# Loading four row tiles of x before w_out and keeping half of the residual on chip in the MLP of a one-layer hybrid attention block

## The chip, the cores and the metric

The kernel runs on one core of a Trainium2 chip. A core has a matrix engine (TensorE, PE in the profile, with its weight loads as PEld), a vector engine (VectorE, DVE), a scalar engine (ScalarE, ACT), GpSimd (POOL) and SyncE (SP, which here only issues DMAs). Each takes its instructions in the order of the program, and they wait for each other by semaphores. On-chip memory is SBUF; matrix products land in PSUM, which has 8 banks of 128 x 512 float32. The metric is the device time of one execution in microseconds, lower is better. Before the change it is 2884.75 us, the median of 3 runs (2883.74 to 2885.79).

## The reference

One layer of a decoder block in float32, 512 positions of 2048 features:

```python
xn = rmsnorm(x, g_mix)
(q_a, k_c, ..., c_q, c_kv, k_r, gate_a, gate_b) = split(xn @ w_in)
o_a = nsa_attention(...)          # 16 heads, compressed, selected and windowed keys
o_b = mla_attention(...)          # 16 heads, low-rank queries and keys
mixed = sigmoid(gate_a) * (o_a @ w_o_nsa) + sigmoid(gate_b) * (o_b @ w_o_mla)
h = x + mixed @ w_out
h = h + memory_cross_attention(rmsnorm(h, g_xattn), rmsnorm(mem, g_mem))   # 4 heads, 256 tokens
h = h + square(relu(rmsnorm(h, g_mlp) @ w_ff1)) @ w_ff2                    # 2048 -> 8192 -> 2048
return rmsnorm(h, g_final)
```

Every matrix is read from memory once, in float32. The change touches `mixed @ w_out`, the cross-attention's output projection, and the MLP.

## The kernel before

**Products.** Each float32 operand is split into a high and a low part in a reduced format. A product is three matmuls: high by high, high by low, low by high (L395 to L397 in the attention stages, L1606 to L1608 in w_out and the MLP). ACT makes the high part by a cast (L402, L1428), DVE the low part by a subtraction (L403, L1433).

**Stages, in order.** The input projection with the first attention, the second attention with the gates (both up to about 1100 us), then `mix` (L1152): the product with w_o_nsa, the memory's keys and values, and a loop over d = 0 to 15 with w_o_mla (L1186 to L1196). Then `Out.run` (L1832), the product with w_out; `cross` (L1280), the cross-attention, whose last part is a loop over four column blocks f of the output projection with four steps k each (L1330 to L1360); and `Mlp.run` (L1529), first w_ff1 (layer 1), then w_ff2 (layer 2).

**The seven products.** w_out and both MLP layers use a fast 2 x 2 block scheme: 7 products instead of 8 for each chunk of weights. w_out has 2 chunks (products p = 0 to 13), each MLP layer 8 chunks (p = 0 to 55 and 56 to 111). A product has four units j = 0 to 3, and a unit is one weight tile of 128 x 1024 (512 KB) with 12 matmuls. Unit i = 4p + j. What a product needs:

- Its weights. `load` (L1407): products n = 0, 3, 5 of a chunk load a tile plainly by SP (L1416). Products 1, 2, 4, 6 add the next block onto the tile that is already there, by an accumulating DMA of POOL (L1423). Such a load can start only when the low part of the unit four before has been made from the same tile.
- High and low parts of the weights: `high` on ACT (L1428), `low` on DVE (L1433).
- Its stationary side S: a sum of activation blocks, made by DVE (`add`, L1470, lines L1474 to L1480), and S's high and low part (`stat` and `stat_low`: ACT L1501, DVE L1506; in w_out L1811 and L1816).

`prep(i)` (L1442) sets the order: loads up to i + 5, high parts up to i + 2, low parts up to i + 1. It is called with i + 3 at unit i. `ahead(step)` makes the same preparations for the first units, in four steps, before the first product starts. In w_out these are called at d = 12 to 15 of the w_o_mla loop (L1195), in the MLP at k = 0 to 3 of the last column block (L1357).

**PSUM.** Four banks are named mm, three st, one o. In w_out the set X is st and o, the set Y is mm. In MLP layer 1 (two banks in a set) X is mm and Y is st (L1544, L1546). The four column blocks of the output projection each use all four mm banks; DVE empties them into the residual at L1349.

**The residual.** h is held as eight tiles `R[t, b]` (four row tiles t, two column halves b) of 128 x 1024. `Out.run` loads x into them by SP (`Out.res_in`, L1828 to L1830): two ahead of the first product, the other six at j = 2 and 3 of products 0 to 2 (L1855). The output projection adds to them. Then:

- `x_in(d)` (L1656) turns the residual to features by four PE transposes (L1261) into an st bank and scales it into the MLP's input, half by ACT (L1659) and half by DVE (L1660). d = 0 to 11 come in the column blocks f = 1 to 3, d = 12 to 15 in product 0 of the MLP (L1567).
- `square(t, q)` (L1743) adds up squares for the norm on ACT, for a row tile and a quarter of the columns.
- `res_out(b)` (L1662) stores four tiles to memory with DMAs issued by ACT (L1664). b = 0 is stored at f = 2, k = 2, b = 1 in product 0 at j = 1. All eight come back by SP in products 39 to 53 (`res_in`, L1678 to L1680).

**Slots.** Nearly everything lives in 40 slots of 128 x 1024 (`Slots`), plus a few lent areas (the tiles named d and PP in the profile). `get` takes the slot that has been free the longest, so an instruction that fills a slot waits for its former readers. Scratch for squares and for u is six half slots (L1397).

**The u transposes.** The MLP's inner result is turned by PE (L1672) into the bank o, copied by ACT (L1673) and stored (L1674), in jobs spread over the next two products.

Of the kernel before, what the change touches and what calls it, by code (L numbers as in the profile page):

```python
# [9 lines left out]
F32 = mybir.dt.float32  # L10
# [344 lines left out]
class Layer:  # L355
    def __init__(self, tc, ctx, a, order, info):
# [17 lines left out]
        self.d_r = dr.tile([4, 2, 128, 1024], F32, name="d_r")  # L374
# [777 lines left out]
    def mix(self):  # L1152
# [32 lines left out]
        out = None  # L1185
        for d in range(KT):  # L1186
            ps = self.ft("wm", d, M)
            g = st[d % 4]
            nc.vector.scalar_tensor_tensor(g, g, 1.0, ps, op0=OP.add, op1=OP.mult)
            nc.vector.tensor_add(self.RES[d], self.RES[d], g)  # L1190
            sig(KT + d + 3)
            if d == 9:
                out = Out(self)
                out.loads(4)
            if d >= 12:  # L1195
                out.ahead(d - 12)  # L1196
# [83 lines left out]
    def cross(self, rate, out):  # L1280
# [49 lines left out]
        for f in range(4):  # L1330
            ps = [self.new_mm() for _ in range(4)]
            for h in range(2):
                w = self.W.get(("xo", f, h))
                for kk in range(2):
# [5 lines left out]
                    for t in range(4):  # L1340
# [4 lines left out]
                        if f and 0 < k < 3 and t % 2:  # L1345
                            mlp.x_in(4 * f + 2 * k - 6 + t // 2)
# [3 lines left out]
                    if f and k == 0:  # L1350
                        for t in range(4):
                            mlp.square(t, f - 1)
                    if f == 2 and k == 2:
                        mlp.res_out(0)
                    if f == 2 and k == 3:
                        mlp.loads(4)
                    if f == 3:  # L1357
                        mlp.ahead(k)
# [7 lines left out]
class Mlp:  # L1366
# [19 lines left out]
    def begin(self, k):  # L1386
# [3 lines left out]
        self.nl = self.nh = self.no = self.ns = 0  # L1390
        self.units = 4 * (self.NP + 7 * self.CH)

    def __init__(self, k):
# [3 lines left out]
        self.us, self.usl = k.halves(6)  # L1397
# [131 lines left out]
    def run(self, out):  # L1529
# [8 lines left out]
        back = deque((t, b) for b, ts in ((0, (0, 1)), (1, (2, 3, 0, 1)), (0, (2, 3))) for t in ts)  # L1538
        for p in range(last):
# [3 lines left out]
            if n == 0:  # L1543
                X = [k.new_mm() for _ in range(nb)]  # L1544
            if n in (1, 5):
                Y = [k.new_st() for _ in range(min(nb, 3))] + [k.new_o() for _ in range(nb - 3)]  # L1546
            ps = (X, Y)[which]
            nh = 1 if p + 1 >= self.NP else 2
            for j in range(4):
# [4 lines left out]
                if j == 1 and back and p > self.NP - 18 and p % 2:  # L1554
                    self.res_in(*back.popleft())
# [9 lines left out]
                if p == 0 and j < 2:  # L1565
                    for d in (0, 1):
                        self.x_in(12 + 2 * j + d)  # L1567
                    if j:
                        for t in range(4):
                            self.square(t, 3)  # L1570
                        self.res_out(1)
                if p == 2 and j == 1:
# [79 lines left out]
    def scratch(self):  # L1652
        self.ns = (self.ns + 1) % 2
        return self.us[4 + self.ns]

    def x_in(self, d):  # L1656
        k, nc = self.k, self.nc
        ps, g = k.to_features(d, k.new_st()), k.gains[:, G_MLP + d:G_MLP + d + 1]
# [3 lines left out]
    def res_out(self, b):  # L1662
        for t in range(4):
            self.nc.scalar.dma_start(self.k.d_r[t, b], self.R[t, b])  # L1664
            self.k.put(self.R.pop((t, b)))
# [12 lines left out]
    def res_in(self, t, b):  # L1678
        self.R[t, b] = self.k.slots.plain()
        self.nc.sync.dma_start(self.R[t, b], self.k.d_r[t, b])  # L1680
# [62 lines left out]
    def square(self, t, q):  # L1743
        self.nc.scalar.activation(self.scratch(), self.row(t, q), AF.Square,
# [27 lines left out]
class Out(Mlp):  # L1772
# [6 lines left out]
    def __init__(self, k):  # L1779
# [5 lines left out]
        self.us = [None] * 4 + [self.own[:, :512], self.own[:, :512]]  # L1785
        self.cols = self.own[:, 512:]
# [41 lines left out]
    def res_in(self, t, b):  # L1828
# [3 lines left out]
    def run(self):  # L1832
# [3 lines left out]
        rows = deque((t, b) for a, b in ((0, 0), (1, 1), (0, 1), (1, 0)) for t in (2 * a, 2 * a + 1))  # L1836
        for _ in range(2):
            self.res_in(*rows.popleft())
        X = Y = None
        for p in range(last + 1):  # L1840
# [6 lines left out]
            for j in range(4):  # L1847
# [7 lines left out]
                if rows and j > 1 and p != 3 and p != 4:  # L1855
                    self.res_in(*rows.popleft())
# [76 lines left out]
```

## Time and profile before

| | us |
|---|---|
| median of 3 runs | 2884.75 (2883.74 to 2885.79) |
| the profiled execution | 2884.82 |
| its span, first to last instruction | 2883.0 |
| mean granted clock of TensorE | 0.997 of full speed |
| TensorE (matmul) busy | 2829.2, 98% |
| VectorE busy | 1927.7, 67% |
| ScalarE busy | 1488.0, 52% |
| GpSimd busy | 385.5, 13% |
| moved by DMA | 459.06 MB, mean 159 GB/s |

The durations in the profile are of one execution. A row of a group gives line, engine, operation, tile written and read, and count. In a row of waits, the engine and what it was about to do stand left of the arrow, what it waited for stands right, then the total, the number of times and the longest in us. A DMA has an issue on its engine's queue and lands later. Matmuls are pipelined, so two neighbours overlap in the records and the busy time of TensorE counts a stream without holes as full.

### The profile page before, as it was taken

The page shows a single profiled execution, that of the slowest core. Times are in us where ns is not written, and L with a number is a line of the kernel's source. Part 1 is how long each engine was busy: PE and PEld are TensorE (multiplying, and loading weights), DVE is VectorE, ACT ScalarE, POOL GpSimd, SP SyncE. Part 2 cuts the span into 40 slices and gives each one's busy share as a digit, 9 for nine tenths or more (in the row PEclk, how much of TensorE's full clock was granted, in tenths as well). Part 3 has the DMA queues.
Part 4 walks back from the last instruction along what each step waited for, and adds up shares of the span by engine and source line. Part 5 has one row for each costly group of instructions (what it writes and reads, how often), then busy time and mean ns, then how long its engine had stood idle before and what let it go on. Part 6 is the DMA issues. An engine that isn't in the chain of part 4 may idle for free. (4 is left out here: it accounts for less than half of the span.)

```text
span 2883.0 us, 37043 instructions
## 1 busy us (share of the span) xinstructions
PE 2829.2 (98%) x13594; PEld 2357.0 (82%) x13594; DVE 1927.7 (67%) x3208; ACT 1488.0 (52%) x2574; POOL 385.5 (13%) x606
## 2 busy tenths in 40 slices
PE   9999999999999999999999999999999999999998
PEld 7878888888888888887887778888887888888886
DVE  6446766655555565457866777777766778888888
ACT  5435555654454444333555566666666544444445
POOL 3121011001010002001200111111111111111110
PEclk9999999999999999999999999999999999999999
DMA  5231111122223335558823788988899888899986
GB/s 175 88 94 61 56 57 59 61 86 98 95 99 99 95 125 195 178 186 229 205 63 110 175 206 204 221 200 200 224 224 241 223 217 224 225 232 226 230 221 163
DMA packets 149141, 459.06 MB, mean 159 GB/s; under 512 B 15840, under 2 KB 32352, under 8 KB 148960
## 3 DMA queue, kind: packets, MB, share of 16 engines
q0 software_dynamic: 41472, 151.01, 27.9%
q1 hardware_dynamic: 81872, 271.88, 27.7%
q10 hardware_dynamic: 25616, 33.82, 3.3%
q8 instruction: 106, 1.74, 0.2%
q14 instruction: 75, 0.61, 0.1%
HBM read 418.90 MB, written 37.75 MB: 158 GB/s over the span
## 5 line engine op out<-in xcount | busy, mean ns | idle before, releaser
L395 PE MATMUL mm<-s,s 128*128 128x512 f32 (+5 forms) x1528 | 609.1, 399 | 9.7 <-ACT s L402 5.8
L397 PE MATMUL mm<-s,s 128*128 128x512 f32 (+5 forms) x1528 | 585.0, 383 | 0.0
L396 PE MATMUL mm<-s,s 128*128 128x512 f32 (+5 forms) x1528 | 584.5, 383 | 0.1
L403 DVE TENSOR_TENSOR s<-s,s 128x512 fp32r<-128x512 f32 (+4 forms) x446 | 304.8, 700 | 228.8 <-ACT s L402 227.2
L1433 DVE TENSOR_TENSOR s<-d,s 128x1024 fp32r<-128x1024 f32 x281 | 339.7, 1222 | 173.4 <-ACT s L1428 173.3
L1606 PE MATMUL mm<-s,s 128*128 128x512 f32 x1120 | 440.8, 394 | 3.3 <-ACT s L1501 2.0
L1428 ACT CAST s<-d 128x1024 fp32r<-128x1024 f32 x281 | 289.4, 1050 | 297.2 <-DMA d<-wts 265.7
L1607 PE MATMUL mm<-s,s 128*128 128x512 f32 x1120 | 436.8, 390 | 1.9 <-DVE s L1433 1.8
L1608 PE MATMUL mm<-s,s 128*128 128x512 f32 x1120 | 437.4, 391 | 1.1 <-DVE s L1506 0.6
L402 ACT CAST s<-s 128x512 fp32r<-128x512 f32 (+4 forms) x446 | 264.1, 608 | 203.9 <-PE mm L396 80.5
L395 PEld LDWEIGHTS mm<-s,s 128*128 128x128 f32 x1528 | 289.4, 189 | 56.5 <-ACT s L402 6.1
L397 PEld LDWEIGHTS mm<-s,s 128*128 128x128 f32 x1528 | 288.1, 189 | 53.8
L396 PEld LDWEIGHTS mm<-s,s 128*128 128x128 f32 x1528 | 289.9, 190 | 37.7 <-DVE s L403 0.9
L1606 PE MATMUL st<-s,s 128*128 128x512 f32 x768 | 301.2, 392 | 0.8 <-ACT s L1811 0.8
L1607 PE MATMUL st<-s,s 128*128 128x512 f32 x768 | 299.2, 390 | 1.5 <-DVE s L1433 1.5
L1608 PE MATMUL st<-s,s 128*128 128x512 f32 x768 | 299.3, 390 | 0.6 <-DVE s L1816 0.6
L1423 POOL DMA_DIRECT2D d<-wts x193 | 168.5, 873 | 872.7 <-DVE s L1433 449.2
L1433 DVE TENSOR_TENSOR s<-s,s 128x1024 fp32r<-128x1024 f32 x185 | 223.4, 1221 | 82.6 <-ACT s L1428 79.3
L1428 ACT CAST s<-s 128x1024 fp32r<-128x1024 f32 x185 | 190.3, 1049 | 143.7 <-DMA s<-wts 127.7
L543 ACT ACTIVATE PP<-PP,mx 128x512 f32<-128x512 f32 (+1 forms) x208 | 116.4, 560 | 278.9 <-DVE mx L542 278.8
L1606 PEld LDWEIGHTS mm<-s,s 128*128 128x128 f32 x1120 | 210.8, 188 | 46.6 <-ACT s L1501 2.4
L1608 PEld LDWEIGHTS mm<-s,s 128*128 128x128 f32 x1120 | 210.6, 188 | 46.4 <-DVE s L1506 1.5
(298 smaller groups left out, 4254.0 us busy)
## 6 DMA issues: line engine op xcount, KB each, us to landing
s<-wts SPq DMA_DIRECT2D x286, 512.0 KB, 3.7
d<-wts POOLq DMA_DIRECT2D x193, 512.0 KB, 9.6
d<-wts SPq DMA_DIRECT2D x88, 512.0 KB, 5.7
s<-wts POOLq DMA_DIRECT2D x70, 512.0 KB, 7.9
d_u<-s ACTq DMA_DIRECT2D x64, 256.0 KB, 5.5
d<-d_u SPq DMA_DIRECT2D x26, 512.0 KB, 5.7
PP<-wts POOLq DMA_DIRECT2D x25, 512.0 KB, 9.6
d_g<-s ACTq DMA_DIRECT2D x32, 256.0 KB, 2.0
```

The costliest lines, as they stand in the source:

```text
L395: t.matmul(ps, a.hr, b.hr, start=first, stop=False)
L396: t.matmul(ps, a.hr, b.lr, start=False, stop=False)
L397: t.matmul(ps, a.lr, b.hr, start=False, stop=last)
L402: nc.scalar.copy(o.hr, src)
L403: nc.vector.tensor_sub(o.lr, src, o.hi)
L543: nc.scalar.activation(p, p, AF.Exp, bias=mx, scale=-1.0, accum_out=sm)
L1423: self.nc.gpsimd.dma_start(t, src, accum_op=OP.add)
L1428: self.nc.scalar.copy(t.hr, self.raw[i])
L1433: self.nc.vector.tensor_sub(t.lr, r, t.hi)
L1606: m(ps, a.hr, b.hr, start=first, stop=False, skip_group_check=True)
L1607: m(ps, a.hr, b.lr, start=False, stop=False, skip_group_check=True)
L1608: m(ps, a.lr, b.hr, start=False, stop=last, skip_group_check=True)
```

## The change

- **w_out.** `Out.res_in` becomes `row_in`. Four of the eight loads of x are issued in the w_o_mla loop, at d = 10, 11, 13 and 14, and the other four at j = 3 of products 0 to 3.
- **Stores.** Only the halves b = 0 are stored and loaded back. The four stores are issued by SP, one each at f = 2, k = 2 and 3, and f = 3, k = 0 and 1. The halves b = 1 keep their slots. The four reloads stay in products 47, 49, 51 and 53.
- **First preparations.** The first four weight tiles of the MLP are loaded at f = 1, k = 3 instead of f = 2, k = 3; `ahead` runs at f = 2, k = 3 and f = 3, k = 0 to 2, one k step sooner.
- **Banks.** In the first chunk of layer 1 X is st and Y is mm. The four `x_in` in product 0 use mm banks.
- **Squares.** Two of the third quarter's squares move from f = 3 to product 0, the four of the last quarter from product 0 to product 1; their sum is taken one unit later. The scratch is `rbc`, which is free by then, and the half slots go from six to four.

The diff, cut to its core:

```diff
-        self.d_r = dr.tile([4, 2, 128, 1024], F32, name="d_r")
+        self.d_r = dr.tile([4, 128, 1024], F32, name="d_r")
...
+            if d in (10, 11, 13, 14):
+                out.row_in()
             if d >= 12:
                 out.ahead(d - 12)
...
-                            mlp.x_in(4 * f + 2 * k - 6 + t // 2)
+                            mlp.x_in(4 * f + 2 * k - 6 + t // 2, self.new_st())
...
                     if f and k == 0:
-                        for t in range(4):
+                        for t in range(4 if f < 3 else 2):
                             mlp.square(t, f - 1)
-                    if f == 2 and k == 2:
-                        mlp.res_out(0)
-                    if f == 2 and k == 3:
+                    if f == 2 and k > 1 or f == 3 and k < 2:
+                        mlp.res_out((k - 2) % 4)
+                    if f == 1 and k == 3:
                         mlp.loads(4)
-                    if f == 3:
-                        mlp.ahead(k)
+                    if f == 2 and k == 3 or f == 3 and k < 3:
+                        mlp.ahead((k + 1) % 4)
...
-        self.us, self.usl = k.halves(6)
+        self.us, self.usl = k.halves(4)
+        self.sq = k.rbc
...
-                X = [k.new_mm() for _ in range(nb)]
+                X = [k.new_mm() if p else k.new_st() for _ in range(nb)]
             if n in (1, 5):
-                Y = [k.new_st() for _ in range(min(nb, 3))] + [k.new_o() for _ in range(nb - 3)]
+                Y = [k.new_st() if p > 6 else k.new_mm() for _ in range(min(nb, 3))] + [k.new_o() for _ in range(nb - 3)]
...
-                if j == 1 and back and p > self.NP - 18 and p % 2:
-                    self.res_in(*back.popleft())
+                if j == 1 and p in (self.NP - 9, self.NP - 7, self.NP - 5, self.NP - 3):
+                    self.res_in((p - self.NP + 9) // 2)
...
-                        self.x_in(12 + 2 * j + d)
-                    if j:
-                        for t in range(4):
-                            self.square(t, 3)
-                        self.res_out(1)
-                if p == 2 and j == 1:
+                        self.x_in(12 + 2 * j + d, k.new_mm())
+                if p == 0 and j == 3:
+                    self.square(2, 2)
+                    self.square(3, 2)
+                if p == 1:
+                    self.square(j, 3)
+                if p == 2 and j == 2:
                     self.r = self.rstd(range(4), "rx3")
...
-    def res_out(self, b):
-        for t in range(4):
-            self.nc.scalar.dma_start(self.k.d_r[t, b], self.R[t, b])
-            self.k.put(self.R.pop((t, b)))
+    def res_out(self, t):
+        self.nc.sync.dma_start(self.k.d_r[t], self.R[t, 0])
+        self.k.put(self.R.pop((t, 0)))
...
-        rows = deque((t, b) for a, b in ((0, 0), (1, 1), (0, 1), (1, 0)) for t in (2 * a, 2 * a + 1))
-        for _ in range(2):
-            self.res_in(*rows.popleft())
...
-                if rows and j > 1 and p != 3 and p != 4:
-                    self.res_in(*rows.popleft())
+                if p < 4 and j == 3:
+                    self.row_in()
```

More of the change, by code (lines that the diff above doesn't have):

```diff
@@ L1389, in begin @@
         self.S, self.sums, self.m = {}, {}, None
[L1390 removed]
+        self.nl = self.nh = self.no = 0
         self.units = 4 * (self.NP + 7 * self.CH)
@@ L1537, in run @@
         last = 2 * self.NP - 1
-        back = deque((t, b) for b, ts in ((0, (0, 1)), (1, (2, 3, 0, 1)), (0, (2, 3))) for t in ts)
         for p in range(last):
@@ L1650, in half, with x_in @@
         return self.us[self.nu % 4]
[L1652 to L1656, printed above, removed]
+    def x_in(self, d, ps):
         k, nc = self.k, self.nc
-        ps, g = k.to_features(d, k.new_st()), k.gains[:, G_MLP + d:G_MLP + d + 1]
+        ps, g = k.to_features(d, ps), k.gains[:, G_MLP + d:G_MLP + d + 1]
         nc.scalar.activation(self.x(d, 0), ps[:, :256], AF.Copy, scale=g)
         nc.vector.tensor_scalar(self.x(d, 1), ps[:, 256:], g, None, op0=OP.mult)
-    def res_out(self, b):
-        for t in range(4):
-            self.nc.scalar.dma_start(self.k.d_r[t, b], self.R[t, b])
-            self.k.put(self.R.pop((t, b)))
+    def res_out(self, t):
+        self.nc.sync.dma_start(self.k.d_r[t], self.R[t, 0])
+        self.k.put(self.R.pop((t, 0)))
     def u_T(self, c, b, j, cs, last):
@@ L1676, in u_T, with res_in @@
             k.put(*cs)
-    def res_in(self, t, b):
-        self.R[t, b] = self.k.slots.plain()
-        self.nc.sync.dma_start(self.R[t, b], self.k.d_r[t, b])
+    def res_in(self, t):
+        self.R[t, 0] = self.k.slots.plain()
+        self.nc.sync.dma_start(self.R[t, 0], self.k.d_r[t])
     def row(self, t, q):
@@ L1743, in square @@
     def square(self, t, q):
-        self.nc.scalar.activation(self.scratch(), self.row(t, q), AF.Square,
+        self.nc.scalar.activation(self.sq, self.row(t, q), AF.Square,
                                   accum_out=self.cols[:, 4 * t + q:4 * t + q + 1])
@@ L1784, in __init__ @@
         self.own = k.slots.get()
-        self.us = [None] * 4 + [self.own[:, :512], self.own[:, :512]]
-        self.cols = self.own[:, 512:]
+        self.sq, self.cols = self.own[:, :512], self.own[:, 512:]
+        self.rows = deque((t, b) for a, b in ((0, 0), (1, 1), (0, 1), (1, 0)) for t in (2 * a, 2 * a + 1))
     def finish(self):
@@ L1826, in ahead, with row_in @@
         self.prep(step - 1)
-    def res_in(self, t, b):
+    def row_in(self):
+        t, b = self.rows.popleft()
         self.R[t, b] = self.k.slots.get()
```

## The prediction

> **What bounds the kernel now.** I read the page first, for who is busy, then a table by stretches, to see where the matmul stream has holes, then the waits of TensorE in those stretches, and last the timelines of the engines it waited for. From the page:
>
> ```profile
> span 2883.0 us, 37043 instructions
> PE 2829.2 (98%) x13594; PEld 2357.0 (82%) x13594; DVE 1927.7 (67%) x3208; ACT 1488.0 (52%) x2574; POOL 385.5 (13%) x606
> q0 software_dynamic: 41472, 151.01, 27.9%
> q1 hardware_dynamic: 81872, 271.88, 27.7%
> ```
>
> TensorE is the bound: it is idle for 2883.0 - 2829.2 = 53.8 us, and the change takes no matmul away. So all it can win is holes, in the stages that it touches. The two queue lines give the price of a 512 KB transfer. POOL's accumulating loads: 27.9% of 2883.0 us is 804 us for 151.01 MB, that is 2.8 us of all 16 DMA engines each. Plain ones: 799 us for 271.88 MB, 1.54 us each.
>
> The stretches (columns: length, busy time and instructions of each engine, granted clock, DMA share, GB/s):
>
> ```profile
> 1285.00:1305.00 20.00, 20.00 (x90) 16.57 (x89) 11.40 (x18) 8.16 (x11) 0.00 (x0) 1.00 0.43 147
> 1305.00:1345.00 40.00, 37.79 (x162) 29.68 (x161) 25.94 (x31) 12.05 (x13) 7.12 (x8) 1.00 1.00 271
> 1330.00:1350.00 20.00, 16.70 (x66) 11.70 (x65) 14.22 (x15) 8.75 (x9) 1.74 (x2) 1.00 0.87 262
> 1400.00:1450.00 50.00, 50.00 (x222) 41.42 (x221) 42.15 (x45) 25.19 (x33) 9.63 (x11) 1.00 0.91 211
> 1580.00:1590.00 10.00, 9.38 (x38) 7.60 (x39) 3.42 (x7) 6.00 (x13) 0.00 (x0) 0.83 0.17 68
> 1600.00:1630.00 30.00, 26.91 (x120) 21.02 (x118) 18.41 (x19) 13.96 (x24) 5.23 (x6) 1.00 0.98 253
> 1630.00:1640.00 10.00, 8.30 (x28) 6.47 (x29) 7.84 (x12) 8.12 (x11) 0.86 (x1) 0.83 0.13 15
> ```
>
> An undisturbed stretch of w_out is 1400 to 1450: 222 matmuls in 50 us, 0.225 us each. Between 1330 and 1350, early in w_out, there are 66 where 20 / 0.225 = 88.8 would fit: 22.8 x 0.225 = 5.1 us lost. The second place is the end of the cross-attention's output projection and the first products of the MLP, 1578 to 1660. There two stretches also have a granted clock of 0.83: 10 x 0.17 = 1.7 us each, 3.4 us. What TensorE waited for, in w_out (1328 to 1352):
>
> ```profile
> PE st L1607 <- DVE s L1433: 1.5, 2, 0.8
> PE st L1606 <- ACT s L1811: 0.8, 1, 0.8
> PE st L1608 <- DVE s L1816: 0.6, 1, 0.6
> PE mm L1608 <- DVE s L1816: 0.3, 1, 0.3
> ```
>
> and from 1575 to 1665:
>
> ```profile
> PE mm L395 <- DVE s L1349: 2.2, 1, 2.2
> PE mm L1606 <- ACT s L1501: 2.0, 1, 2.0
> PE mm L1606 <- DVE s L1349: 1.2, 1, 1.2
> PE st L1261 <- DVE d L1660: 1.2, 1, 1.2
> PE mm L1607 <- DVE s L1433: 1.1, 2, 0.8
> PE mm L1608 <- DVE s L1506: 0.6, 1, 0.6
> ```
>
> In w_out the waits are 3.2 us in 5 gaps and the loss 5.1, so a gap costs its length and up to 0.4 us of emptying and refilling. In the second place the waits are 8.3 us in 7 gaps, the low clock 3.4, and for the refilling I take 0.2 each, 1.4: 13.1 us.
>
> **The change, part by part.**
>
> Four row tiles ahead of w_out. All 8 loads of x now fall into the stretch where the DMA engines are full. The loads, ACT's waits from 1310 to 1346, and the landing of POOL's accumulating loads (L1423) in it:
>
> ```profile
> L1830 SPq DMA_DIRECT2D s<-xr x8: 328/355/488, 1310.4 to 1341.2; - x8
> ```
>
> ```profile
> ACT s L1428 <- DMA d<-wts: 14.5, 4, 5.7
> ACT s L1428 <- DMA PP<-wts: 6.9, 2, 5.1
> ```
>
> ```profile
> DMA to landing us min/median/max: 7.3/11.2/14.4
> ```
>
> ACT waits 21.4 us for accumulated weights, and TensorE's four kinds of wait stand behind that queue: L1433 and L1816 on DVE and L1811 on ACT come after L1428 in program order. From 1305 to 1345 the share is 1.00, and the eight rows take 8 x 1.54 = 12.3 us of these 40. Four of them move to d = 10, 11, 13, 14 of the w_o_mla loop, about 1282 to 1306, where the share is 0.43; the fifth to eighth go one to a product, so that the last two fall behind 1340. On SP they stand behind gate loads that are already waiting there, and the slots they take were freed before that loop began (by the code's order of gets and puts). Behind a later row that waits for a slot stand the plain weight loads of the fourth product, which are asked for 8 units (21.6 us) ahead. So 6.2 us leave the full stretch for certain and up to 3 more go to its end, against 5.1 us of lateness. I take 4.6 of 5.1 (bounds: 2.5, if the accumulating loads stay late because each waits for its predecessor's L1433; 5.1). Extra cost in the earlier stage: 6.2 us of DMA time into 0.57 x 20 = 11.4 us of free time, nothing.
>
> Stores off ACT. Before, four d_r stores are issued by ACT in the third column block (timelines of ACT, then DVE):
>
> ```profile
> 1575.68 2.91 ACTq L1664 DMA_DIRECT2D d_r<-s  x4
> 1578.63 0.62 ACT L402 CAST s<-s 128x512 fp32r<-128x512 f32 x1 [2.48 <-issue]
> ```
>
> ```profile
> 1579.28 0.69 DVE L403 TENSOR_TENSOR s<-s,s 128x512 fp32r<-128x512 f32 x1 [2.61 <-ACT s L402]
> ```
>
> Four issues hold ACT for 2.91 us, the weight split at L402 waits, DVE's L403 waits for that, and the evacuation at L1349 stands behind L403: that is the 2.2 us wait of L395. After it the clock is 0.83. With SP issuing the stores one at a time this chain is gone. SP has only weight loads behind it there, and the stored halves have been complete for a column block. Worth 2.2 + 1.7 + 0.2 = 4.1 us (bounds: 2.4, without the clock; 4.1).
>
> Banks. The first product takes st banks, which no L1349 evacuates: the 1.2 us wait of L1606 goes, 1.4 with refilling. The four x_in transposes inside product 0 take mm banks, four of them instead of three that are reused: the 1.2 us of L1261 goes, 1.4. Products 1 to 6 then use mm for Y; these banks are emptied in product 0, whose 48 matmuls take 10.8 us. What is late next is DVE. This is its row for the low parts:
>
> ```profile
> L1433 DVE TENSOR_TENSOR s<-d,s 128x1024 fp32r<-128x1024 f32 x281 | 339.7, 1222 | 173.4 <-ACT s L1428 173.3
> ```
>
> Product 0 holds eight operations of this size on DVE (four lows, two sums, two low parts of S), 9.8 us, and eight of at most half of it (four L1349, four x_in), at most 4.9: 14.7 us against 10.8 and the transposes. Lows are made three units ahead, 3 x 12 x 0.225 = 8.1 us, which covers the 4 us. Nothing added; 4 us if that lead is used up.
>
> First preparations sooner, second four stores dropped. In products 1 and 2 the chain is the same as in w_out. Landing of POOL's loads issued 1590 to 1597, then of those issued 1605 to 1622, and the stores:
>
> ```profile
> DMA to landing us min/median/max: 5.4/5.7/5.9
> ```
>
> ```profile
> DMA to landing us min/median/max: 11.9/13.5/14.9
> ```
>
> ```profile
> d_r<-s ACTq DMA_DIRECT2D x4, 512.0 KB, 17.0
> ```
>
> The loads need 13.5 us where the first two needed 5.7, at a DMA share of 0.98, and four stores (6.2 us) are in the same stretch. After the change these stores do not exist, the first weights come a column block (10.8 us) earlier, and the accumulating loads one k step (12 matmuls, 2.7 us) earlier against product 0. ACT also loses four issues and two of four squares from product 0; four squares go to product 1, one to a unit. What this chain costs is the waits of L1606 for L1501, of L1607 and of L1608, the second low clock, and 0.2 for each of four gaps: 2.0 + 1.1 + 0.6 + 1.7 + 0.8 = 6.2 us; I take 5.3 off (bounds 2.5 and 6.2). The one scratch for all squares is written by ACT alone, in order, and rstd, one unit later, is first used at the end of product 3: nothing.
>
> Half of the residual kept. Four reloads fewer before layer 2 and the same number of stores saved above. TensorE's waits from 1665 to 2260 are mainly these:
>
> ```profile
> PE o L1672 <- ACT s L1673: 8.7, 9, 2.2
> ```
>
> ```profile
> ACT s L1428 <- DMA d<-wts: 42.3, 25, 4.0
> ACT s L1428 <- PE mm L1608: 1.9, 1, 1.9
> ```
>
> ```profile
> 2199.50 0.44 PE L1672 MATMUL o<-cst,PP 128*128 128x128 f32 x2 [2.25 <-ACT s L1673]
> ```
>
> ```profile
> 2200.00:2205.00 5.00, 5.00 (x24) 4.13 (x23) 2.48 (x3) 3.86 (x6) 0.00 (x0) 1.00 0.52 162
> ```
>
> (The ACT lines are from 1700 to 2050; then one matmul group of the timeline, and the stretch behind it.) The u transposes wait because ACT's copy stands behind an accumulated load. The remaining four reloads stay where the biggest of them is, at 2199, so I credit 0.4 us (bounds: -3, if three slots fewer in hand delay something in each of 8 column chunks; +2).
>
> Sum: 4.6 + 4.1 + 1.4 + 1.4 + 5.3 + 0.4 = 17.2 us. The profiled execution took 2884.82 us with its span of 2883.0, so 1.8 us lie around the span, and the median of the three runs is 2884.75. The span becomes 2865.8, the time 2867.6.
>
> **The rivals.**
>
> Smaller gain, DMA still binding. If the accumulating loads are late for their order (each waits for the low part of the unit four before) and not for traffic, w_out gives 2.5 and the MLP's start 2.5: 17.2 - 2.1 - 2.8 = 12.3, time 2872.5. For it: POOL's landings rise to 14.4 us. Against: from 1400 on the order is the same, with no hole.
>
> Given back. TensorE arrives 17 us earlier at products whose u transposes already wait. If each of the 8 chunks loses 0.7 us more, 5.6 us return: 2873.2. For it: ACT's 42.3 us of waits for accumulated weights. Against: the start of a chunk does not depend on when the stage began.
>
> The low clock stays. The 2.2 us gap at 1578 is followed by a clock of 0.83, but the 2.25 us gap before 2199.50 by one of 1.00. If the low stretches are not the gaps' doing, 3.4 us stay: 2871.0. The Trainium skill ("TensorE: Matmul & The Clock Gate", Part 1) lets the clock fall after at least one idle window of about 3.4 us, longer than any gap here; by that rule the sum would be 13.8 and this rival would hold. The trace speaks against it, since both low stretches begin right at a gap of about 2 us.
>
> Slower, by lack of slots. Kept rows take four slots and the scratch gives one back. Counting the code's gets and puts, 8 slots of 40 are free in products 2 to 4 of each chunk before; that becomes 5, and 3 in the first chunk. It decides when the slot that a unit four places ahead gets was last read by the unit just before TensorE's own. Twelve such units in 8 chunks at 0.3 us would be 29 us: 2896.4. The Trainium skill ("Perfetto Trace Analysis", Optimization Strategy) reads the same gap repeating as too few buffers, and would look for it here. Against it: w_out's second chunk goes down to 2 free slots by the same count and shows 222 matmuls in 50 us (1400 to 1450), and ACT waited only once for TensorE to free a slot from 1700 to 2050, 1.9 us.
>
> The change does not do what it says: SP's stores stand behind its other loads, the four early rows wait for slots, and what remains is the banks' 2.8 us: 2882.
>
> **How the numbers follow.** Forecast 0.56; DMA still binding 0.14; given back 0.12; low clock 0.08; nothing but banks 0.06; slower 0.04. A measurement of this kernel tells about 0.2% from no change, 5.8 us. All cases but the last two are faster by more: 0.90; same 0.06; slower 0.04. The range: at its best 5.1 + 4.1 + 2.8 + 6.2 + 2 = 20.2 us, 2864.6, and 1 us more for gaps I have priced low, 2863.5; at the other end the cases down to 2873.2 with 2 us for two of them together, 2875.5.
>
> **What would show it.** Right: L1830 starts near 1282 and has four issues before 1307; from 1330 to 1350 some 88 matmuls; no wait of L395 for L1349 near 1578; no granted clock under 1 from 1570 to 1640; no L1261 wait for L1660; landings of POOL's loads in product 1 under 10 us; the L1672 waits still about 8 us. Wrong: L1672's waits over 14 us, ACT's L1428 waiting for L1608 in every chunk, a new wait of L395 in the w_o_mla loop for late weights, or TensorE's first MLP matmul waiting for L1660 on the st banks.

## The result, and the profile after

The changed kernel takes 2866.07 us, the median of four runs (2863.43 to 2869.15); the kernel before took 2884.31 us beside it. The ratio is 0.9933, 95% interval [0.9922, 0.9945]: 19.3 us less, between 15.9 and 22.5. The profiled execution took 2866.99 us with a span of 2865.2, 17.8 us shorter than the span before. The forecast was 17.2 us.

From the page of the changed kernel:

```profile
span 2865.2 us, 37061 instructions
PE 2824.7 (99%) x13594; PEld 2358.1 (82%) x13594; DVE 1929.0 (67%) x3208; ACT 1488.9 (52%) x2574; POOL 384.2 (13%) x606
```

TensorE is idle for 40.5 us, 53.8 before. The rest of the gain is in its busy time, 4.5 us less: records of matmuls that run at a low clock, or whose start is held back, count as busy. So I also count the loss in another way: for every 128 x 512 matmul, how much later than 0.2267 us the next one starts, summed by stretch. This count is worked out from the timelines of TensorE and used below for all kernels:

| lost time, us | before | changed | difference | over all kernels | forecast |
|---|---|---|---|---|---|
| 1300 to 1500, w_out | 6.56 | 5.28 | 1.3 | 0.4 | 4.6 |
| 1560 to 1665, output projection and first MLP products | 14.55 | 1.94 | 12.6 | 11.2 | 12.2 |
| 1665 to 2280, rest of layer 1 | 17.36 | 13.69 | 3.7 | 7.3 | 0.4 |
| all else | 41.19 | 42.89 | -1.7 | not compared | 0 |

Two profiles are one execution each, and the count of a stretch in which nothing was edited moves by 1 to 3 us from one to the next. The twelve experiments below give more of them, so the fifth column compares means. In w_out, six kernels without the edit lose 6.39 to 6.73 (mean 6.55), four with it 5.06 to 7.72 (6.20). From 1560 to 1665, four kernels with none of the edits there lose 11.48 to 14.55 (13.18), five with all of them 1.94 to 2.03 (2.00). In the rest of layer 1, four with all slots in hand lose 17.36 to 21.10 (19.27), seven with three slots fewer 10.71 to 13.69 (11.98). That sums to 18.9 us, beside the 19.3 measured. (In the two profiles alone the four rows sum to 15.9 of the 17.8 us; the rest lies in what the count leaves out, such as the smaller matmuls.) The means also hold stretches of low clock, some 1.5 us each, which come in some executions and not in others: from none to two in the four kernels of 13.18, and one in w_out in one of the four of 6.20.

So the total came out as forecast, and one of its three parts did. w_out gave almost nothing of its 4.6 us, and layer 1 gave about 7 where 0.4 was forecast.

The stretches of the changed kernel, with the columns of the forecast's table:

```profile
1285.00:1305.00 20.00, 20.00 (x89) 16.55 (x89) 11.13 (x16) 8.79 (x12) 0.00 (x0) 1.00 0.69 242
1305.00:1345.00 40.00, 38.79 (x170) 31.43 (x169) 28.78 (x33) 12.96 (x13) 7.10 (x8) 1.00 0.90 237
1330.00:1350.00 20.00, 18.45 (x79) 14.27 (x78) 14.27 (x15) 10.01 (x10) 2.53 (x3) 1.00 0.73 195
1580.00:1590.00 10.00, 10.00 (x53) 8.28 (x53) 5.58 (x8) 5.74 (x9) 1.75 (x2) 1.00 0.37 56
1600.00:1630.00 30.00, 30.00 (x134) 24.85 (x133) 25.03 (x29) 22.86 (x36) 5.27 (x7) 1.00 0.77 170
1630.00:1640.00 10.00, 10.00 (x46) 8.29 (x45) 9.96 (x10) 4.35 (x5) 3.47 (x4) 1.00 0.96 202
```

Three stretches are whole now: 53 matmuls where there were 38, 134 for 120, 46 for 28, and both low clocks (0.83) are gone. From 1330 to 1350 there are 79, not the 88 that I had named as the sign of a closed hole. What TensorE still waits for, first in w_out (1328 to 1385), then from 1665 to 2260; from 1545 to 1665 the view lists no wait at all:

```profile
PE st L1610 <- DVE s L1436: 1.2, 2, 0.8
PE mm L1610 <- DVE s L1436: 0.8, 1, 0.8
PE mm L1611 <- DVE s L1814: 0.3, 1, 0.3
PE mm L1609 <- ACT s L1431: 0.2, 1, 0.2
...
PE o L1670 <- ACT s L1671: 4.5, 3, 1.9
```

(Line numbers have shifted: L1609 to L1611 are the matmuls, L1431 the high part on ACT, L1436 the low part on DVE, L1426 POOL's accumulating load, L1419 the plain load, L1829 the row of x, L1670 and L1671 the u transposes and their copy.) The waits for the u transposes are 4.5 us in 3 places, where they were 8.7 in 9.

Why w_out gained so little is seen in three answers. The first is the landing of POOL's accumulating loads that are issued between 1305 and 1342, before 11.1 us in the median; the second are the rows of x; the third is ACT's timeline at a hole that was not there before:

```profile
DMA to landing us min/median/max: 7.0/10.4/11.4
```

```profile
L1829 SPq DMA_DIRECT2D s<-xr x8: 328/369/384, 1283.4 to 1358.7; - x8
```

```profile
1376.60 1.05 ACT L1431 CAST s<-s 128x1024 fp32r<-128x1024 f32 x1 [6.55 <-DMA s<-wts]
1377.55 1.04 ACT L1431 CAST s<-PP 128x1024 fp32r<-128x1024 f32 x1
1378.50 1.06 ACT L1809 ACTIVATE s<-d 128x1024 fp32r<-128x1024 f32 x1
```

Four rows did leave, as said, for the time before 1307. But the DMA engines stay nearly full (0.90 from 1305 to 1345), and the landing falls by 0.7 us only. And the last row goes out at 1358.75, where its slot comes free; the plain load behind it goes out at 1361.25 and lands after 15.3 us, ACT waits 6.55 us for it, and TensorE loses about 1.4 us at 1377.

### The profile page after: what moved, and what is told of

Its sections match the earlier page's. It is cut to its first block, busy times and chain, and to the rows that moved or that the text cites. A ratio compares the mean times of both kernels' runs of the same rounds, so it can differ in the third digit from the quotient of the medians.

```text
span 2865.2 us, 37061 instructions
## 1 busy us (share of the span) xinstructions
PE 2824.7 (99%) x13594; PEld 2358.1 (82%) x13594; DVE 1929.0 (67%) x3208; ACT 1488.9 (52%) x2574; POOL 384.2 (13%) x606
## 4 chain that ended last, share of the span: by engine, by line
PE 61%; issue 16%; DMA 10%; DVE 7%; ACT 4%; POOL 3%; POOLq 0%; ACTq 0%; SPq 0%; DVEq 0%
PE mm L395 12%; PE mm L397 12%; PE mm L396 12%; DMA d<-wts 6%; DMA s<-wts 3%; PE mm L1610 3%; PE mm L1611 3%; PE mm L1609 3%; POOL d L1426 2%; DVE s L1436 2%; PE st L1611 2%; PE st L1609 2%; PE st L1610 2%; PE st L616 2%; PE o L634 1%
## 5 line engine op out<-in xcount | busy, mean ns | idle before, releaser
L1436 DVE TENSOR_TENSOR s<-d,s 128x1024 fp32r<-128x1024 f32 x281 | 339.6, 1221 | 157.4 <-ACT s L1431 157.2
L1609 PE MATMUL mm<-s,s 128*128 128x512 f32 x1104 | 434.2, 393 | 0.2 <-ACT s L1431 0.2
L1610 PE MATMUL mm<-s,s 128*128 128x512 f32 x1104 | 430.4, 390 | 1.9 <-DVE s L1436 1.9
L1431 ACT CAST s<-d 128x1024 fp32r<-128x1024 f32 x281 | 289.1, 1049 | 275.3 <-DMA d<-wts 240.2
L1611 PE MATMUL mm<-s,s 128*128 128x512 f32 x1104 | 430.6, 390 | 0.3 <-DVE s L1814 0.3
L1609 PE MATMUL st<-s,s 128*128 128x512 f32 x784 | 307.6, 392 | 0.0
L1610 PE MATMUL st<-s,s 128*128 128x512 f32 x784 | 305.2, 389 | 1.2 <-DVE s L1436 1.2
L1611 PE MATMUL st<-s,s 128*128 128x512 f32 x784 | 305.4, 390 | 0.0
L1426 POOL DMA_DIRECT2D d<-wts x193 | 168.4, 873 | 864.5 <-DVE s L1436 605.4
L1436 DVE TENSOR_TENSOR s<-s,s 128x1024 fp32r<-128x1024 f32 x185 | 223.3, 1221 | 84.0 <-ACT s L1431 83.8
L1431 ACT CAST s<-s 128x1024 fp32r<-128x1024 f32 x185 | 190.1, 1049 | 144.3 <-DMA s<-wts 134.4
L1611 PEld LDWEIGHTS mm<-s,s 128*128 128x128 f32 x1104 | 207.7, 188 | 44.5 <-DVE s L1814 0.8
```

Source lines behind the costliest of these rows:

```text
L1426: self.nc.gpsimd.dma_start(t, src, accum_op=OP.add)
L1431: self.nc.scalar.copy(t.hr, self.raw[i])
L1436: self.nc.vector.tensor_sub(t.lr, r, t.hi)
L1609: m(ps, a.hr, b.hr, start=first, stop=False, skip_group_check=True)
L1610: m(ps, a.hr, b.lr, start=False, stop=False, skip_group_check=True)
L1611: m(ps, a.lr, b.hr, start=False, stop=last, skip_group_check=True)
```

## The experiments

Ratios are to the kernel before on the same chip, with the 95% interval. The first four make one part of the change, or one thing that it does on the side, alone in the kernel before; the next four take a part away from the changed kernel or shift one; the last four ask what was still open.

**The w_out part alone.** In the kernel before, only the rows of x are moved.

```diff
+            if d in (10, 11, 13, 14):
+                out.row_in()
...
-                if rows and j > 1 and p != 3 and p != 4:
-                    self.res_in(*rows.popleft())
+                if p < 4 and j == 3:
+                    self.row_in()
```

> The kernel before with the w_out part alone: four row tiles of x in the w_o_mla loop, the other four one to a product. Theory A (the trace of the changed kernel): the accumulating loads in w_out still share the DMA engines with the plain weight loads and two rows, and a later row that waits for a slot holds up a plain load behind it, so only 1 to 2 us are gained: 2882.5 to 2883.5. Theory B (the prediction's term): 4.6 us, 2879.7, with no hole between 1330 and 1380.

Measured 2884.53 us, ratio 0.9993 [0.9985, 1.0002]: 2 us or nothing. The loss in w_out is 5.06 us, and the same holes as in the changed kernel stand at 1338 to 1346 and at 1376. The forecast's 4.6 us falls.

**The stores alone.** In the kernel before, all eight stores of the residual are issued by SP instead of ACT.

```diff
-            self.nc.scalar.dma_start(self.k.d_r[t, b], self.R[t, b])
+            self.nc.sync.dma_start(self.k.d_r[t, b], self.R[t, b])
```

> The kernel before with all eight residual stores issued by SP instead of ACT, at the same places, nothing else. The chain of the prediction (four issues on ACT, then the split, then DVE, then the evacuation): the 2.2 us wait at 1578 and the low clock behind it go, 4.1 us, and ACT saves another 2.9 us in product 0, worth up to 1 more: 2879 to 2880.7. Rival: the wait is caused by the stores' traffic or by something else on DVE, then under 1 us changes: 2884.

Measured 2878.44 us, 0.9970 [0.9957, 0.9982], 8.7 us less (between 5.2 and 12.4); the loss from 1560 to 1665 is 6.23, against the mean of 13.2. Two stretches, and what TensorE still waits for from 1545 to 1665:

```profile
1580.00:1590.00 10.00, 10.00 (x54) 8.30 (x53) 3.40 (x7) 7.28 (x15) 0.86 (x1) 1.00 0.00 1
1630.00:1640.00 10.00, 9.77 (x43) 7.59 (x42) 8.91 (x14) 7.05 (x10) 3.35 (x4) 1.00 0.81 168
```

```profile
PE mm L1606 <- DVE s L1349: 1.2, 1, 1.2
PE st L1261 <- DVE d L1660: 1.2, 1, 1.2
...
PE mm L1608 <- DVE s L1506: 0.6, 1, 0.6
PE mm L1606 <- ACT s L1501: 0.5, 1, 0.5
PE mm L1607 <- DVE s L1433: 0.3, 1, 0.3
```

The wait of 2.2 us at 1578 is gone, and both low clocks. And the wait for L1501 fell from 2.0 to 0.5 us, though all eight rows are still stored. Holding ACT does not explain this second part. The first casts behind the later four stores (L1428, L1501) start at 1609.60 and 1610.56 before and at 1606.64 and 1607.60 here, in a kernel that is 3.1 us ahead at this point: with the stores off its queue ACT waits 1.07 us for weights there, where it waited 0.89 us behind the stores. What changed is when the stores move. They go out at 1593 instead of 1607 and have all landed by 1604; before, they landed from 1618 to 1632, beside POOL's loads for products 1 and 2. The landing of the same five of those loads, before, then here:

```profile
DMA to landing us min/median/max: 11.5/13.1/14.9
```

```profile
DMA to landing us min/median/max: 9.8/11.1/11.9
```

So the first four stores cost by holding ACT, the second four, as far as these times tell, by their traffic; no run moved the second four alone. I had credited moving the stores with the first half of this only.

**Half of the residual kept, alone.** In the kernel before, the second four stores and their four reloads are left out, the halves keep their slots; three slots fewer go round in layer 1.

```diff
-                        self.res_out(1)
...
-                if j == 1 and back and p > self.NP - 18 and p % 2:
-                    self.res_in(*back.popleft())
+                if j == 1 and p in (self.NP - 9, self.NP - 7, self.NP - 5, self.NP - 3):
+                    self.res_in((p - self.NP + 9) // 2, 0)
```

> The kernel before, with the column half b = 1 of the residual kept on chip: its four stores in product 0 and four reloads are gone, three fewer slots are free in layer 1, the scratch is the shared one; stores of b = 0 stay on ACT, banks and preparations as before. Theory A: the stores' traffic and their issues on ACT make most of the late loads in products 1 and 2, so 4 to 6 us there, and the u transposes wait less, 2 to 4 us: 2875 to 2878. Theory B (prediction): preparations and stores together 5.3, of these at least half by the stores, and 0.4 in the chunks: 2880 to 2881.5. Lack of slots would show as more waits of the u transposes and a time above 2884.

Measured 2870.60 us, 0.9944 [0.9932, 0.9957], 16.2 us less, the largest of the parts and more than either theory gave. Waits of TensorE, 1545 to 1665, then 1665 to 2260:

```profile
PE mm L395 <- DVE s L1349: 2.3, 1, 2.3
PE st L1261 <- DVE d L1659: 1.2, 1, 1.2
PE mm L1605 <- DVE s L1349: 1.2, 1, 1.2
...
PE o L1671 <- ACT s L1672: 2.9, 7, 1.2
```

Of the first products only the three waits are left that belong to ACT's first four stores and to the banks. That half the forecast had. The other half is new: the u transposes wait 2.9 us instead of 8.7, all through layer 1, also where no reload is near. Either the dropped transfers or the missing slots do this; the next run holds slots and drops nothing.

**Three slots fewer, and nothing else.** In the kernel before, three slots lie idle from product 4 to product 38.

```diff
+                if p == 4 and j == 0:
+                    self.held = [k.slots.get() for _ in range(3)]
+                if p == 38 and j == 0:
+                    k.put(*self.held)
```

> The kernel before with three slots taken out of use from product 4 to product 38 of MLP layer 1, nothing else. Theory A1: with fewer slots the plain loads are issued later and share the DMA engines less with the accumulating ones, so the waits for the u transposes fall from 8.7 us towards 4.5 and the time to about 2880. Theory A2: those waits have nothing to do with slots, time 2884 and waits 8 to 9 us. Theory S (the slower rival of the prediction): they rise, above 2890.

Measured 2877.20 us, 0.9966 [0.9954, 0.9979], 9.8 us less, by taking space away. The loss from 1665 to 2280 is 13.03, against the mean of 19.3 with all slots: 6.3 us. What changes is when SP's plain loads go out in a chunk. Before, then with three slots held (that kernel is 3.9 us ahead here):

```profile
1774.18 0.84 SPq L1416 DMA_DIRECT2D s<-wts  x2
1779.86 0.33 SPq L1416 DMA_DIRECT2D s<-wts  x1
1786.00 0.33 SPq L1416 DMA_DIRECT2D s<-wts  x1
```

```profile
1770.30 0.33 SPq L1417 DMA_DIRECT2D s<-wts  x1
1776.20 0.33 SPq L1417 DMA_DIRECT2D s<-wts  x1
1779.16 0.33 SPq L1417 DMA_DIRECT2D s<-wts  x1
1782.16 0.33 SPq L1417 DMA_DIRECT2D s<-wts  x1
```

With a slot at hand two loads go out together, and share the DMA engines with the accumulating loads that ACT waits for. With none at hand the second goes out 5.9 us after the first. That fewer slots shorten the waits and the time is shown. That it is by this spacing is only argued from the issue times, as no run spaced the loads with all slots in hand, and the landings give it little support: from 1665 to 2037 the median for POOL's accumulating loads is 9.1 us before and 9.2 with three slots held, and in the chunk shown the load that ACT waits for longest needs 13.6 us instead of 13.8. The remaining 3.5 us of the gain are within the interval.

**Banks as before, in the changed kernel.**

```diff
-                X = [k.new_mm() if p else k.new_st() for _ in range(nb)]
+                X = [k.new_mm() for _ in range(nb)]
...
-                        self.x_in(12 + 2 * j + d, k.new_mm())
+                        self.x_in(12 + 2 * j + d, k.new_st())
```

> The changed kernel with the banks as before: X on mm and Y on st in the first chunk, x_in of product 0 on st. Prediction's term: the wait of the first MLP matmul for the evacuation (1.2 us) and the x_in wait (1.2) come back, with refilling 2.8 us lost, gain over the kernel before about 15 us. Rival: since DVE and ACT have less to do there now, the banks are free in time and nothing is lost (gain 18).

Measured 2865.29 us, 0.9925 [0.9912, 0.9938]: no slower than the changed kernel. In the profile the wait of the first product for L1351 is back, 1.2 us, and the loss from 1560 to 1665 is 3.26 instead of 2.0. The wait of the transposes for x_in's copy does not come back. So the banks are worth 1.3 us in the profile, not 2.8, and nothing that the time can tell.

**First preparations at their old place, in the changed kernel.** The loads are issued at f = 2, k = 3, and `ahead(k)` at f = 3.

> The changed kernel with the first preparations at the old places (weights at f = 2, k = 3, the four steps at f = 3, k = 0 to 3). Theory A: dropping the stores and taking them off ACT did most, and 0 to 1.5 us are lost. Theory B (half of the prediction's term for late loads): 2.5 to 3 us lost, with waits of TensorE for L1436 and L1504 in products 1 and 2 again.

Measured 2868.47 us, 0.9938 [0.9927, 0.9950]. The time can't tell it from the changed kernel. In the profile the waits for the low parts are back (2.6 us for L1436 and L1509), as Theory B has it, and the loss from 1560 to 1665 is 5.96 us, 4.0 more than with the earlier preparations. Other stretches, in which nothing was edited, differ by 2.4 us both ways.

**All eight rows before w_out, in the changed kernel.**

```diff
             if d in (10, 11, 13, 14):
                 out.row_in()
+                out.row_in()
...
-                if p < 4 and j == 3:
-                    self.row_in()
```

> The changed kernel with all eight row tiles of x loaded in the w_o_mla loop, two at each of d = 10, 11, 13, 14, none in the products. Theory A (w_out's holes are DMA time: 6 accumulating loads, 4 plain ones and 2 rows fill the 26 us from 1316 to 1342, and one row in SP's queue holds up a plain load that is late at 1377): the holes at 1377 (1.5 us) and at least half of the 2.4 us at 1340 go, 2.5 to 4 us faster than the changed kernel. Theory B (accumulating loads have a rate of their own, 3.8 us each, whatever else moves): only the 1377 hole goes, 1.5 us, and the landings stay 3.8 us apart.

Measured 2860.02 us, 0.9912 [0.9899, 0.9925]: some 6 us less than the changed kernel by the two ratios, though their intervals just overlap. In the profile w_out loses 3.5 us less, as Theory A has it.

**w_out's weights and preparations one step d sooner, in the changed kernel.**

```diff
-            if d == 9:
+            if d == 8:
...
-            if d >= 12:
-                out.ahead(d - 12)
+            if d >= 11:
+                out.ahead(d - 11)
```

> The changed kernel with w_out's first weights and preparations one d (24 matmuls, 5.4 us) sooner, rows where the change has them. Both theories of w_out's holes give the accumulating loads 5.4 us more lead, so the 2.4 us at 1340 go; the hole at 1377 stays, as its plain load stands behind a row in SP's queue: 2 to 2.5 us faster than the changed kernel. Rival: the accumulating loads start no sooner, because each waits for a low part that stands in DVE's order between the work of the w_o_mla loop: no change.

Measured 2858.55 us, 0.9907 [0.9894, 0.9920], a gain over the changed kernel, as the intervals just fail to touch. The same stretches of the last two kernels, first with all rows moved, then with the earlier weights:

```profile
1305.00:1345.00 40.00, 40.00 (x178) 32.91 (x176) 30.77 (x34) 15.06 (x16) 7.76 (x9) 1.00 0.82 210
1330.00:1350.00 20.00, 19.87 (x88) 16.10 (x88) 16.10 (x19) 8.47 (x10) 2.59 (x3) 1.00 0.68 168
```

```profile
1305.00:1345.00 40.00, 40.00 (x178) 33.13 (x177) 31.11 (x34) 16.43 (x17) 7.02 (x9) 1.00 0.92 252
1330.00:1350.00 20.00, 20.00 (x89) 16.54 (x89) 16.54 (x19) 8.58 (x9) 3.36 (x4) 1.00 0.79 209
```

Both close the holes, by different means: 88 and 89 matmuls from 1330 to 1350, no wait of TensorE from 1328 to 1385, a loss in w_out of 1.8 and 1.3 us instead of 5.28. Moving eight rows takes traffic out (share 0.82). Starting sooner leaves the DMA engines as full as they were (0.92) and gives the loads 5 us more; the landings of POOL's loads are 8.3 us in the median where the changed kernel has 10.4. In w_out the wait is one of lateness under traffic, and half of either remedy was too little. The plain load that made the hole at 1377 still takes 14.2 us and ACT still waits 6.6 us for it, but it goes out at 1357.15 instead of 1361.25, and the hole is gone. Of the 7.5 us between this time and the changed kernel's some 4 to 5 are w_out's; the rest I can't place.

**Six slots held instead of three, in the kernel before.**

> The kernel before with six of its slots held idle between products 4 and 38 of layer 1 (instead of the three of the earlier experiment, which made it 0.9966). Theory A (fewer slots put SP's second plain load behind a release, so that it no longer shares the DMA engines with the accumulating load that is needed next): the gain of the three slots stays or grows a little, 0 to 3 us beyond it, ratio 0.9955 to 0.9970, waits of the u transposes between products 4 and 38 below 2 us in sum. Theory B (the forecast's slower case, lack of slots, only begins later than thought): with two slots to pass round, loads come after they are wanted, new waits of the MLP's matmuls for the high parts (L1433) of 0.3 to 1 us a chunk appear, and the time is above that with three held: ratio 0.998 to 1.005.

Measured 2877.82 us, 0.9978 [0.9969, 0.9987]: as far as the intervals tell, no more gain than with three, and less than Theory A gave. But TensorE's waits follow the dose. TensorE's and ACT's waits from 1665 to 2037, about the products in which the slots are held, for none, three and six:

```profile
PE o L1672 <- ACT s L1673: 5.3, 6, 1.5
...
ACT s L1428 <- DMA d<-wts: 41.9, 26, 4.0
```

```profile
PE o L1677 <- ACT s L1678: 1.6, 3, 1.0
...
ACT s L1429 <- DMA d<-wts: 37.7, 27, 3.4
```

```profile
PE o L1677 <- ACT s L1678: 0.6, 2, 0.3
...
ACT s L1429 <- DMA d<-wts: 31.4, 22, 2.8
```

TensorE has no wait for a high or low part in this stretch with two slots left: the lack of slots that the forecast feared did not reach it even there. It does begin on ACT: for SP's plain weight loads ACT waits not at all before, 2.1 us in 2 places with three slots held, and 24.5 us in 13 places with six. What was saved was lost again after product 38, where the slots are free: three waits of 1.3, 1.6 and 2.2 us at 2108 to 2192, and the low clock after the last.

**Three more slots held, on top of the earlier weights of w_out.**

> The changed kernel with w_out's weights one step sooner (2858.55 us, 0.9907) and three more slots held idle between products 4 and 38 of layer 1. Theory A (spacing of loads by slots goes on): the u transposes' waits of 4.5 us in 5 places shrink to about 2, time 2855 to 2857, ratio 0.989 to 0.990. Theory B (the three slots that the kept residual takes have already done what holding slots can do): no change within 1.5 us, ratio 0.9905 to 0.991. Theory C (lack of slots begins): matmul waits for the high parts, 2860 to 2870, ratio above 0.9915.

Measured 2858.54 us, 0.9907 [0.9893, 0.9922], the same as without. The waits of the u transposes fall from 4.5 us in 5 places to 2.5 in 2, but the one that is left is 2.2 us long and is followed by the low clock. Theory B, that the kept residual has already taken what slots can give, holds by the time.

**Only the earlier loads and preparations of the MLP, in the kernel before.**

> The kernel before with only the earlier loads and preparations of the MLP: the first weights are asked for at the end of column tile 1 instead of 2, and the preparations run one step sooner; stores stay with ACT, all eight rows are still stored and read back. Theory A (the forecast's term: DVE's preparations were late by themselves): the four DVE gaps at the MLP's start, 1.4 us in sum, go, and the gap of 2.2 us at 1578 stays, because ACT's stores still stand ahead of what PE waits for: ratio 0.9990 to 1.0000. Theory B (the gap at 1578 comes from ACT's preparations standing behind the stores, so preparing before the stores takes it away as well as moving the stores to SP does): 6 to 9 us, ratio 0.9970 to 0.9980, loss of the stretch 1560 to 1665 near 6 us instead of 14.6. Theory C: the earlier loads collide with the column tiles' weights, slower by 1 to 5 us, 1.0005 to 1.002.

Measured 2880.55 us, 0.9987 [0.9977, 0.9997], with runs from 2876.86 to 2887.08: 3.7 us less, between 0.9 and 6.6. The gap at 1578 stays at 2.2 us, since ACT's stores still stand there; the four waits behind the preparations (L1501, L1506, L1433) are 2.2 us instead of 3.7, and the loss from 1560 to 1665 is 11.76, within what kernels without this edit lose there. It is the forecast's account: small, about 1.4 us of its own, with stores and traffic still in the way.

**The four reloads eight products earlier** (products 39 to 45), on top of the three more slots held.

> As the last but one (w_out's weights one step sooner, three slots held idle in products 4 to 38), and the four reloads of the residual eight products earlier: products 39, 41, 43 and 45 instead of 47, 49, 51 and 53. It asks whether the wait of 2 us that every kernel of this case shows near the end of layer 1 (2199 us before, 2178 in the changed kernel) is the reloads' doing. Theory A: the reload that stands among the plain loads of that chunk makes the accumulated load late; without it the wait goes or falls under 0.8 us, u transposes wait 0.3 to 1.3 us in sum where they waited 2.5, time 2855 to 2857.5. Theory B: the wait belongs to the chunk itself (its three slots are free again there and plain loads go out together): it stays near 2 us, time 2857.5 to 2860. Theory C: the wait only moves with the reloads, to about 2060 to 2110 us.

Measured 2861.25 us, 0.9921 [0.9908, 0.9935]. The time is above what theories A and B gave. The wait near the end of layer 1 falls from 2.2 to 0.9 us, as if the reload had been its cause, and no low clock follows it; but in sum the u transposes wait no less (1.8 us for their copy and 1.2 for the square before it, L1638, where they waited 2.5). Nor does every kernel show a wait of 2 us there: with the half kept alone, or the preparations at their old place, the longest is 1.2. And the time did not follow: in this profile TensorE waits 2.5 us at 2840 for a low part in layer 2, which is far from the edit and also stands in two of the other profiles. Whether these two belong together is open.

## Why the prediction was right, and where its steps were not

The time came as forecast (2867.6 against 2866.07 us), but of the steps only those at the MLP's start held, so the closeness of the total is in part luck.

- **w_out, 4.6 us: mis-sized; 0.4 by the means, 1.3 in the two profiles, 2 or nothing in the time of the part alone.** The step that failed is "6.2 us leave the full stretch for certain and up to 3 more go to its end, against 5.1 us of lateness". It set bytes against lateness as if a microsecond of traffic removed were one of waiting removed. The share fell from 1.00 to 0.90, which is 4 us of DMA time out of 40, and yet the landings only from 11.1 to 10.4 us. This is the smaller-gain rival in w_out alone, without its reason: it was not the order of the loads, for removing the other four rows closes the holes with the order as it was. The last row also made a hole of its own.
- **Stores off ACT, 4.1 us: the mechanism right, its reach too small.** Alone, with all eight stores on SP, it is worth 8.7 us, since the second four also go out sooner and no longer land beside the loads of products 1 and 2.
- **Banks, 2.8 us: mis-sized, 1.3 in the profile.** One of its two waits does not return when the banks are put back.
- **First preparations and dropped stores, 5.3 us: the mechanism right.** POOL's loads for products 1 and 2 land after 8.0 us in the median instead of 13.5, and the three waits behind them are gone. Alone, and against the mean of 13.2, the kept half gives 6.0 us in that stretch, the preparations 1.4 and the moved stores 7.0: 14.4 in sum, where all edits together, banks included, give 11.2. They cure the same waits, and the 1.4 is within what kernels without any of these edits differ by. The sum of 12.2 held because it shared the waits of the profile out among the edits, each once.
- **Half of the residual kept, 0.4 us: the sign of its side effect was wrong.** Layer 1 gained about 7 us (3.7 between the two profiles), beyond the bound of 2; three slots held with all transfers kept gave 6.3 of it. The u transposes, which were to wait about 8 us still, wait 4.5. I had asked what three slots fewer might delay, never what they might hold back to good effect.
- **Low clock.** The sum counted 3.4 us for it, and both low stretches went with their gaps, as the trace had it. But they were not certain: with the w_out part alone the gap of 2.2 us at 1579 stands as before, and the clock behind it is 1.00, with 53 matmuls from 1580 to 1590. One came back, at 2178.77 after a wait of 1.9 us:

```profile
2178.00:2188.00 10.00, 9.23 (x36) 7.56 (x37) 6.89 (x7) 7.82 (x11) 0.86 (x1) 0.83 0.51 137
```

- **The slower rival, lack of slots,** did not come true, neither in the change nor with three or six slots held; with six the lack shows on ACT and not on TensorE. The Trainium skill ("Perfetto Trace Analysis", Optimization Strategy) reads the same gap repeating as a possible sign of too few buffers. Here the gap that repeats in each chunk shrank as slots were taken away: 5.3, 1.6 and 0.6 us in sum.

The two large errors, 4 us too much in w_out and about 7 too little in layer 1, partly cancelled by luck; the total says nothing about either.

## What to carry to other kernels

A queue that computes should not issue transfers just ahead of what the critical engine waits for: price an issue by all that stands behind it, and a transfer by the loads that are under way when it moves. More buffers are not always better: here taking some away shortened TensorE's waits, it seems because a free buffer lets a prefetch go out beside a load that is due. And to judge a part of a change, undo it or make it alone; the sum over parts can come out right with half of its terms wrong.

## What the runs showed of the hardware

**The clock after gaps of about 2 us.** In the fourteen profiles TensorE had 19 waits of 1.9 us or more in the middle of a matmul stream between 1300 and 2860 us. After 12 of them the next 6 to 8 matmuls start about 0.427 us apart instead of 0.227, 1.2 to 1.6 us lost; after 7 they don't, one of them 2.48 us long. After none of the waits between 1.3 and 1.9 us did it happen.

The length of the gap is not the whole of it. The traces hold the times at which the granted clock changes. In every one of them these lie on a grid of 3.41 us: in the kernel before, the clock is full for 418, 14 and 363 times 3.41 us between its low stretches, and the low stretches at 1581 and 1632 last 3.41 us each. So look at TensorE's idle time in each step of the grid. Two pairs of steps of the kernel before, each a step with a gap and the step behind it (columns as in the tables above: length, busy time of TensorE, ..., clock):

```profile
1577.83:1581.24 3.41, 1.18 (x6) 0.64 (x5) 1.96 (x4) 1.19 (x3) 0.00 (x0) 1.00 1.02 407
1581.24:1584.65 3.41, 3.41 (x10) 2.66 (x9) 1.12 (x2) 3.41 (x10) 0.00 (x0) 0.50 0.14 52
2195.64:2199.06 3.42, 1.61 (x8) 0.99 (x6) 1.01 (x1) 2.09 (x3) 0.00 (x0) 1.00 1.04 281
2199.06:2202.47 3.41, 2.97 (x15) 2.56 (x16) 1.59 (x3) 1.71 (x3) 0.00 (x0) 1.00 0.84 262
```

The gap of 2.23 us before 1580.62 falls into one step, and the next step has half the clock. The gap of 2.25 us before 2199.50 is divided, 1.81 and 0.44 us, and the clock stays. In the fourteen profiles, from 1300 us to the end, every step in which TensorE was idle for 1.92 us or more is followed by half the clock, and of the steps with 1.91 us or less only one: 1.63 us, at 1375 in the kernel with the preparations at their old place, after two waits of 0.9 and 0.8 us. In the earlier stages the idle time, as the profile models it, does not divide the steps so cleanly: near 489 us two steps with 1.17 us are followed by half the clock. One step at half the clock costs at most half of 3.41 us, 1.7, as a clock of 0.83 over 10 us says too.

The Trainium skill ("TensorE: Matmul & The Clock Gate", Part 1) speaks of an idle window of about 3.4 us that runs freely. The traces agree with a window of this length that runs freely, but not with one that has to be idle throughout: 1.92 us of idle time in it were enough.

**Issuing has a price where something stands behind it.** Four stores took ACT 2.91 us to issue at 1575.68, and with them on SP the wait of 2.2 us behind them is gone. The later four, issued from 1607.53 to 1609.56 while ACT worked on squares, held up nothing that would have started sooner. The Trainium skill ("DMA: Bandwidth & Descriptors", Issuing engines are not separate DMA queues) holds that issuing elsewhere saves sequencer time that is usually small beside the transfer. Here it was 2.91 us beside some 6.2 us of transfer (four times 1.54), on an engine that TensorE waits for.
